# Two more seven-product joints in the middle of each layer, with the residual read again from DRAM

## The chip, the cores and the metric

One Trainium2 chip, one core. The time is the device time of one execution in microseconds. The kernel before takes 917.99 us (median of 3 runs, 916.48 to 919.03).

## The reference

A two-layer encoder on one sequence of 256 tokens with 2048 features, in float32. Cut to what matters:

```
for l in range(2):
    h = rmsnorm(x)                                  # 256 x 2048
    P = h @ w_in[l]                                 # 2048 x 7168, columns:
    a_x, a_b, a_c, a_g, d_q, d_k, d_v, d_g, m_q, m_g = split(P)
    #  768  768  768  768  768  768  768  768  512  512
    y_a = a_b * conv3(a_c * a_x) * silu(a_g)
    y_d = head_rms(diff_attention(norm(d_q), norm(d_k), d_v)) * silu(d_g)   # 6 heads, two softmaxes each
    y_m = mem_attention(norm(m_q), mem keys, mem values) * silu(m_g)        # 4 heads, 256 memory tokens
    x = x + concat(y_a, y_d, y_m) @ w_out[l]        # 2048 x 2048, the residual is x
```

## The kernel before

**Products.** TensorE (PE) works in fp32r, in which an fp32 number is split into a rounded part `hi` and a rest `lo`. Each fp32 product of a 128-token tile, a 128-row weight tile and 512 columns is three matmuls: hi·hi, hi·lo and lo·hi. `block` goes down the 16 row tiles of a weight matrix for 512 columns, two row tiles (a chunk) at a time. For each chunk SP issues a load of 512 KB into `raw` (a ring of 4, line L276), ACT rounds it into `hi` (L279), DVE subtracts to get `lo` (L280), both into a ring of 4 chunks, and PE does 12 matmuls (two row tiles, two token tiles, three each) at L290. Two accumulators of PSUM are used by a block.

**Seven products instead of eight.** For a pair of row tiles and two neighbouring column blocks, the function `seven` does a 2x2 block product with 7 products in place of 8 (21 matmuls of 512 columns for 24). It needs the following in return: two `wide` tiles (one row tile by 1024 columns each) in place of four ring chunks' halves; four subtractions of wide halves on DVE (`minus`, L365); splits of one half (`one`) and of three whole tiles (L362); sums of token tiles (`token_sums`), which are kept in rows 12 to 15 of `yT`, where the outputs of the four memory heads go later; and four more PSUM banks, x1 and x5 of pool `ps_s`, x6 and x7 of pool `ps_t`. These four are the banks that attention scores and attention outputs use at other times. A `joint` runs a block of the near columns with sevens put in at given row tiles (its `places`), then `collect` (L1048) adds x1, x6, x7 and x5 into four results `u`, and then the far columns' block runs on the row tiles that are left. `gather` (L1075) adds the `u` to the accumulators. Before, there are 10 sevens: in w_in in layer 0 one at place 8 of the first joint and two at 2 and 10 of the second, in layer 1 two at 4 and 10, all of them in the d columns at the layer's start; and five in w_out (2 and 3).

**Order of the program.** A layer's blocks of w_in are the d columns (six blocks), then the middle: C_M (memory queries), C_M+512 (memory gate), C_B, one with the rests of C_B and C_G, C_G, C_X, then C_C, and one with the rests of C_X and C_C. Then comes w_out. Beside the blocks run tasks: after each chunk `run_side` moves every task that is due (score and softmax of a pair of heads, normalisation, transposes, gates) by one step. A transpose goes through DRAM on SP's queue (`carry`: four writes at L470, such as `d<-sh`, and four reads at L474, such as `bgT<-d`). Most instructions are pinned to the order in which the program issues them; a scheduler orders the others.

**Attention beside it.** `pair` (three of them in each layer) runs two heads: 24 score matmuls (`s`, L582) into four banks of ps_s and ps_t, two `diff_weights` (L594 to L613: subtract the ALiBi, maximum, exp) with two steps between the heads, carry, and `weighted` into ps_t (`po`). Four memory heads follow with scores in ps_s and `po` in ps_t, and the outputs in yT.

**The residual.** `xs` is one resident tile of 128 x 2 x 2048 (16 KB of each partition). It holds mem at first, then x, is added to the w_out sums in place (L1282), and its squares give the next norm. At a layer's end `x_next` writes each quarter of it to DRAM for the transposes of the next layer.

Of the kernel before, what the change touches and what calls it, by code (L numbers as in the profile page):

```python
# [10 lines left out]
F32 = mybir.dt.float32  # L11
# [7 lines left out]
P = 128  # L19
# [5 lines left out]
W_MEM = 512  # L25
# [26 lines left out]
def encoder(ctx: ExitStack, tc: tile.TileContext, x, mem, norm_g, w_in, conv_w, conv_b,  # L52
# [34 lines left out]

    xs = const.tile([P, NT, D_MODEL], F32, name="xs")
    vb = tmp.tile([P, 2, B], F32, tag="yn", name="vb")
# [263 lines left out]
    def seven(stat, k, sums, rows, c_near, c_far, x, first, last, homes, meanwhile, single=(keep, "mga")):  # L353


        a, b = (pl.tile([P, 2, NB], F32, tag=tag, name=nm("wide")) for pl, tag in homes)
        for j, raw in enumerate((a, b)):
            pin(nc.sync.dma_start(raw.rearrange("p j c -> p (j c)"), rows(k + j)))

# [9 lines left out]

        one = single[0].tile([P, 2, 1, NB], F32R, tag=single[1], name=nm("one"))  # L370
        b11 = split(a[:, 0:1], (one[:, 0], one[:, 1]))
# [156 lines left out]

    held = {"e": 0, "sh": 0, "yn": 0}

    def pair(heads, begin, end, v):
# [27 lines left out]
        for i, h in enumerate(heads):  # L559
            end[0](h, yn[:, :, i], weighted(eT, i, v, h), *es[i][1:])  # L560
            yield 2
# [11 lines left out]
    def diff_scores(l, heads, yT):  # L573
        while not {(x, l, h) for x in "qk" for h in heads} <= made:
            yield 1
        scores = [[pl.tile([P, NT, SEQ], F32, tag=tag, name=nm("s")) for _ in range(2)]
                  for pl, tag in ((ps_s, "s"), (ps_t, "t"))]
        for h, s in reversed(list(zip(heads, scores))):
            for i in range(NT):
                for n, (a, b) in enumerate(((0, 1), (0, 0), (1, 0))):  # L580
                    for c, rows in enumerate(ROWS):
                        pin(nc.tensor.matmul(s[c][:, i, :], yT[rows, a, h, i * P:(i + 1) * P], yT[rows, b, CG + h, :],  # L582
                                             start=n == 0, stop=n == 2))
            scored.add((l, h))
        return scores
# [42 lines left out]
    def mem_scores(l, h, st):  # L628
# [8 lines left out]
        pin(nc.vector.scalar_tensor_tensor(kl, k, g, kh.bitcast(F32), ALU.mult, ALU.subtract))  # L637
        yield 1
        s = ps_s.tile([P, NT, SEQ], F32, tag="s", name=nm("s"))
        for i in range(NT):  # L640
# [21 lines left out]
    def mem_pair(l, n, st):  # L662
# [43 lines left out]
        yield 1  # L706
        for i, h in enumerate(heads):
            po = ps_t.tile([P, SEQ], F32, tag="t", name=nm("po"))
            at = 0
# [59 lines left out]
    def x_next(dst, l, q):  # L769

        d = dram.tile([NT, P, NB], F32, name=nm("xd"))
        tc.keep_in_program_order(nc.sync.dma_start(d.rearrange("t p c -> p t c"), xs[:, :, q * NB:(q + 1) * NB]))
        yield 2
        yield from x_turned(dst, l, q, d.rearrange("t p c -> (t p) c"))
# [12 lines left out]
    def x_square(c, t, pin=False):  # L787
        sq = tmp.tile([P, NB], F32, tag="nat", name=nm("sq"), bufs=3)
        i = nc.scalar.activation(sq, xs[:, t, c * NB:(c + 1) * NB], AF.Square, accum_out=ssx[:, t, c:c + 1])  # L789
        if pin:  # L790
            tc.keep_in_program_order(i)
# [8 lines left out]
    def mem_tokens(lo, n):  # L800
        return pin(nc.sync.dma_start(xs[:, :, lo:lo + n], mem[:, lo:lo + n].rearrange("(t p) c -> p t c", p=P)))

    def mem_columns(k, t):
        return xs[:, t, k * P:(k + 1) * P]

    def mem_squares(c):

        for t in range(NT):
            sq = tmp.tile([P, NB], F32, tag="nat", name=nm("msq"), bufs=3)
            pin(nc.scalar.activation(sq, xs[:, t, c * NB:(c + 1) * NB], AF.Square, accum_out=ssm[:, t, c:c + 1]))  # L810

# [24 lines left out]
    def x_natural(q):  # L836
        pin(nc.sync.dma_start(xs[:, :, q * NB:(q + 1) * NB],
                              x[:, q * NB:(q + 1) * NB].rearrange("(t p) c -> p t c", p=P)))
# [184 lines left out]
    for l in range(DEPTH):  # L1023
# [15 lines left out]

        def joint(b, places, homes, singles, home, **how):  # L1040
            near, far = accumulators(), accumulators()
            x = [pl.tile([P, NB], F32, tag=tag, name=nm("x"))
                 for pl, tag in ((ps_s, "s"), (ps_s, "s"), (ps_t, "t"), (ps_t, "t"))]
            u = keep.tile([P, 3, NB], F32, tag=home, name=nm("u"))
            us = [u[:, 0], u[:, 1], u[:, 2], tmp.tile([P, NB], F32, tag="yn", name=nm("u"))]

# [3 lines left out]
            def collect():  # L1050
                x1, x5, x6, x7 = x
                pin(nc.scalar.copy(us[0], x1))
# [4 lines left out]
                plus(us[3], us[1], x5)  # L1057

            def pair_at(n):
                def run(near):  # L1060
                    rows = lambda k: x_row_tiles(w_in[l], k, 1)[:, 0, C_D + b * NB:C_D + (b + 2) * NB]
                    seven(xT, 2 * n, summed[n], rows, near, far, x, n == 0, n == len(places) - 1,
                          homes[n], lambda: None, singles[n])
                    if n == len(places) - 1:
                        tasks.append(later(collect(), 1))
                    run_side(1)
                return run

            x_block([(C_D + b * NB, NB)], ALLK[2 * len(places):], acc=near, opened=(False, False),
                    between={c: pair_at(n) for n, c in enumerate(places)}, **how)  # L1070
            return near, far, us

        def gather(acc, us):
            for t in range(NT):
                nc.vector.tensor_tensor(us[t], acc[t], us[t], ALU.add)  # L1075
            return us

        def begin_pair(n, p):
# [15 lines left out]
        for b in order:  # L1094
# [7 lines left out]
            elif b in joints:  # L1102
                places = joints[b][0]
                acc, far, us = joint(b, *joints[b])
                finish = us[0:2]
            elif b - 1 in joints:
                acc = x_block([(C_D + b * NB, NB)], ALLK[2 * len(places):], acc=far, opened=(True, False))
                finish = us[2:4]
            else:
                acc = x_block([(C_D + b * NB, NB)], ready=m.ready if l == 0 and b == 0 else None)  # L1110

            def sums_of(acc=acc, us=finish):
                return gather(acc, us) if us else acc

# [30 lines left out]
        mga = sheet(keep, "mga")  # L1145
        acc = x_block([(C_M, NB)])

        def turn_mq(steps):
            nat = yield from steps
            yield 1  # L1150
# [3 lines left out]

        tasks.append(later(turn_mq(normed_steps(acc, P, st, sheets("bgx"))), LAG))
        acc = x_block([(C_M + W_MEM, NB)])

        def mem_gate(acc=acc):
            for t in range(NT):
                a = tmp.tile([P, NB], F32, tag="nat", name=nm("a"), bufs=3)  # L1160
# [68 lines left out]

        acc_b = x_block([(C_B, NB)])  # L1230
        soon(lambda: scaled(both_rows(bg, 0, 4), acc_b, HR2))
        acc_bg = x_block([(C_B + NB, 256), (C_G + NB, 256)])

        def last_gates():
            scaled(both_rows(bg, 4, 6), part(acc_bg, 0, 256), HR2)
            gate(NB, 256, part(acc_bg, 256, 256))

        soon(last_gates)
        acc_g = x_block([(C_G, NB)])
        soon(lambda: gate(0, NB, acc_g))  # L1240
        tasks.append(later(turn_bg(list(range(CG))), 9))
        acc_x = x_block([(C_X, NB)])
        ux = sheet(tmp, "e")
        soon(lambda: scaled(both_rows(ux, 0, 4), acc_x, R2))
        acc_c = x_block([(C_C, NB)])
# [27 lines left out]

        accs = [block(yT, w_out[l], [(b * NB, NB)], heads, more=True) for b in range(2)]
        final = l + 1 == DEPTH

        def finish(b, acc, keep_order=lambda i: i):
            for t in range(NT):
                n = 256 if final else NB
                for lo in range(0, NB, n):  # L1280
                    xc = xs[:, t, b * NB + lo:b * NB + lo + n]
                    keep_order(nc.vector.tensor_tensor(xc, acc[t][:, lo:lo + n], xc, ALU.add))  # L1282
# [25 lines left out]
        def collect(near):  # L1308

            def at(t, b):  # L1310
                return xs[:, t, b * NB:(b + 1) * NB]

# [21 lines left out]
        def pair_at(n):  # L1334
            def run(near):
                seven(yT, paired[n], sums[n], lambda k: w_out[l][k * P:(k + 1) * P, 2 * NB:4 * NB], near, far, x, n == 0, n == len(paired) - 1,
                      homes[n], (lambda: leave(1, accs[1], pin, 4)) if n == 0 else lambda: None)
# [40 lines left out]
```

## Time and profile before

| What | Value |
|---|---|
| median of 3 runs | 917.99 us (916.48 to 919.03) |
| the profiled execution | 917.21 us; the trace spans 915.4 us of it |
| granted TensorE clock, mean | 0.999 |
| PE busy | 909.6 us, 99% of the span |
| DVE busy | 672.4 us, 73% |
| ACT busy | 566.7 us, 62% |
| moved by DMA | 215.18 MB, mean 235 GB/s |

Busy times are sums of each engine's instructions. A matmul's record has about 390 ns and the next one starts before it ends, so PE's busy share says that PE has always something under way, and not how fast it is fed; the spacing between two starts tells that. In the chain that ended last, a piece "PE acc L290 x60" stands for sixty consecutive matmuls and their time.

### The profile page before, as it was taken

What the parts mean: (1) busy time and instruction counts of PE and PEld (TensorE: products, weight loads), DVE (VectorE), ACT (ScalarE), POOL (GpSimd) and SP (SyncE); (2) the same over time, 40 slices, a digit from 0 to 9 for tenths busy, and PEclk for the clock granted to TensorE, in tenths of its full rate; (3) what the DMA queues carried; (4) which work ended last, traced back from release to release, by engine and by line L of the source; (5) the groups of instructions that cost most, each with busy time, mean ns of one, the idle gap of its engine ahead of it and who ended that gap; (6) DMA issues with size and microseconds to landing.
All of it is one profiled execution on the core that took longest, in us unless ns stands there. A gap on an engine that the chain in (4) does not pass through costs nothing.

```text
span 915.4 us, 12589 instructions
## 1 busy us (share of the span) xinstructions
PE 909.6 (99%) x4194; PEld 751.5 (82%) x4194; DVE 672.4 (73%) x935; ACT 566.7 (62%) x1107; POOL 129.9 (14%) x187
## 2 busy tenths in 40 slices
PE   9999999999999999999999999999999999999998
PEld 6887888788888888888888888888888888888886
DVE  5558877987667667677689768876677578588786
ACT  5668865757757665545557656676666576456352
POOL 2376242200021010000000202120021010000000
PEclk9999999999999999999999999999999999999999
DMA  8898767777779898978776872887768999978842
GB/s 289 279 267 255 246 246 251 239 219 214 215 216 253 231 259 248 237 229 242 253 217 226 282 276 85 262 269 228 211 204 207 237 285 287 231 247 235 282 152 93
DMA packets 243282, 215.18 MB, mean 235 GB/s; under 512 B 131976, under 2 KB 171720, under 8 KB 243216
## 3 DMA queue, kind: packets, MB, share of 16 engines
q1 hardware_dynamic: 238240, 208.71, 76.5%
q0 software_dynamic: 3776, 4.59, 2.0%
q10 hardware_dynamic: 1200, 1.07, 0.3%
q8 instruction: 33, 0.54, 0.2%
q14 instruction: 33, 0.27, 0.1%
HBM read 193.30 MB, written 21.00 MB: 234 GB/s over the span
## 4 chain that ended last, share of the span: by engine, by line
PE 92%; DMA 2%; ACT 2%; DVE 2%; issue 1%; SPq 0%; ACTq 0%; DVEq 0%
PE acc L290 83%; PE x L336 3%; PE acc L336 2%; DMA raw<-in_w_mem_kv_dram 1%; PE po L491 1%; PE s L582 1%; DMA wide<-in_w_in_dram 1%; PE po L714 1%; DVE lo L280 1%; PE acc L894 1%; ACT sq L789 0%; ACT hi L876 0%; PE pt L728 0%; DMA d<-sh 0%; ACT sq L421 0%
## 5 line engine op out<-in xcount | busy, mean ns | idle before, releaser
L290 PE MATMUL acc<-hi,xT 128*128 128x512 f32 x1712 | 536.7, 390 | 0.0
L280 DVE TENSOR_TENSOR lo<-raw,hi 128x1024 fp32r<-128x1024 f32 x260 | 316.4, 1220 | 139.1 <-ACT hi L279 133.7
L279 ACT CAST hi<-raw 128x1024 fp32r<-128x1024 f32 x260 | 272.5, 1050 | 206.2 <-PE acc L290 164.6
L290 PEld LDWEIGHTS acc<-hi,xT 128*128 128x128 f32 x1712 | 321.3, 188 | 67.1 <-ACT hi L279 0.2
L290 PE MATMUL acc<-lo,xT 128*128 128x512 f32 x856 | 333.6, 390 | 0.3 <-DVE lo L280 0.3
L290 PEld LDWEIGHTS acc<-lo,xT 128*128 128x128 f32 x856 | 160.7, 188 | 32.8 <-DVE lo L280 0.7
L290 PE MATMUL acc<-hi,yT 128*128 128x512 f32 (+1 forms) x432 | 134.2, 388 | 0.0
L290 PEld LDWEIGHTS acc<-hi,yT 128*128 128x128 f32 x432 | 81.0, 188 | 16.8
L290 PE MATMUL acc<-lo,yT 128*128 128x512 f32 x216 | 83.7, 388 | 0.0
L290 PE MATMUL acc<-hi,memT 128*128 128x512 f32 x248 | 78.6, 393 | 0.0
L877 DVE SCALAR_TENSOR_TENSOR lo<-raw,cva,hi 128x1024 fp32r<-128x1024 f32 (+1 forms) x34 | 40.7, 1217 | 22.7 <-ACT hi L876 22.7
L290 PEld LDWEIGHTS acc<-hi,memT 128*128 128x128 f32 x248 | 46.1, 188 | 9.5 <-ACT hi L876 0.3
L290 PE MATMUL acc<-lo,memT 128*128 128x512 f32 x124 | 48.6, 392 | 0.1
L362 ACT CAST hi<-wide 128x1024 fp32r<-128x1024 f32 x30 | 31.2, 1048 | 26.4 <-DVE wide L365 10.7
L290 PEld LDWEIGHTS acc<-lo,yT 128*128 128x128 f32 x216 | 40.6, 188 | 8.4
L362 DVE TENSOR_TENSOR lo<-wide,hi 128x1024 fp32r<-128x1024 f32 x30 | 36.4, 1220 | 6.4 <-ACT hi L362 6.2
L876 ACT ACTIVATE hi<-raw,cva 128x1024 fp32r<-128x1024 f32 (+1 forms) x34 | 36.4, 1097 | 7.2 <-DMA raw<-in_w_mem_kv_dram 6.2
L424 POOL TENSOR_SCALAR ss<-ss,st 128x8 f32<-128x8 f32 (+1 forms) x16 | 14.6, 913 | 130.0 <-ACT sq L421 130.0
L187 POOL TENSOR_TENSOR rs<-ss,root 128x8 f32<-128x8 f32 (+1 forms) x20 | 32.0, 1601 | 1.7
L599 ACT ACTIVATE e<-e,mx 128x256 f32<-128x256 f32 x48 | 23.8, 498 | 9.6 <-DVE mx L594 9.6
L290 PEld LDWEIGHTS acc<-lo,memT 128*128 128x128 f32 x124 | 23.3, 188 | 6.0 <-DVE lo L877 1.2
L402 POOL TENSOR_SCALAR stt<-ssum 128x2 f32<-128x2 f32 x3 | 0.6, 188 | 186.3 <-DVE ssum L778 186.3
(213 smaller groups left out, 903.2 us busy)
## 6 DMA issues: line engine op xcount, KB each, us to landing
raw<-in_w_in_dram SPq DMA_DIRECT2D x182, 512.0 KB, 4.6
raw<-in_w_out_dram SPq DMA_DIRECT2D x54, 512.0 KB, 4.7
raw<-in_w_in_dram SPq DMA_DIRECT2D x64, 256.0 KB, 3.7
raw<-in_w_mem_kv_dram SPq DMA_DIRECT2D x30, 512.0 KB, 5.8
d<-sh SPq DMA_DIRECT2D x88, 128.0 KB, 4.3
sh<-d SPq DMA_DIRECT2D x72, 128.0 KB, 3.8
wide<-in_w_in_dram SPq DMA_DIRECT2D x10, 512.0 KB, 5.9
wide<-in_w_out_dram SPq DMA_DIRECT2D x10, 512.0 KB, 5.9
```

Of the source, the lines that this page charges most:

```text
L187: nc.gpsimd.tensor_tensor(r, t, root[:, 0:n], ALU.pow)
L279: nc.scalar.copy(hi, raw)
L280: nc.vector.tensor_tensor(lo_, raw, hi.bitcast(F32), ALU.subtract)
L290: i = nc.tensor.matmul(acc, left, right, start=start, stop=stop)
L336: nc.tensor.matmul(acc, left[a], right[b], start=first and i == 0, stop=last and i == 2)
L362: return ((hi, pin(nc.scalar.copy(hi, src))), (lo, pin(nc.vector.tensor_tensor(lo, src, hi.bitcast(F32), ALU.subtract))))
L424: nc.gpsimd.tensor_scalar(ss[:, t], ss[:, t], 1.0 / gs, col(st, ET, t), ALU.mult, ALU.add)
L491: nc.tensor.matmul(po[:, t, :], eT[:, i, t, k, :], v[:, k, h * P:(h + 1) * P], start=k == 0, stop=k == NT - 1)
L582: pin(nc.tensor.matmul(s[c][:, i, :], yT[rows, a, h, i * P:(i + 1) * P], yT[rows, b, CG + h, :], start=n == 0, stop=n == 2))
L599: nc.scalar.activation(e[:, c, i], e[:, c, i], AF.Exp, bias=mx[:, c, i:i + 1], scale=-1.0, accum_out=sm[:, c, i:i + 1])
L876: both = (nc.scalar.activation(hi[:, j], raw[:, j], AF.Copy, scale=g), nc.vector.scalar_tensor_tensor(lo[:, j], raw[:, j], g, hi[:, j].bit ...
L877: nc.vector.scalar_tensor_tensor(lo[:, j], raw[:, j], g, hi[:, j].bitcast(F32), ALU.mult, ALU.subtract))
```

## The change

The residual is no longer resident. A pool `quarters` of four tiles (the bytes of `xs`) holds, one after the other, the quarters of mem, the quarters of x for layer 0's squares, and in each layer's middle the wide tiles, the `one` parts and the results `u` of two new joints. Then, after each of the first two w_out blocks, two quarters of the residual are read from DRAM (512 KB each): x itself in layer 0, the copy that `x_next` wrote in layer 1. The new joints are C_M with C_M+512 and C_G with C_X, each with sevens at row tiles 2 and 8, in both layers: 8 sevens more, 18 in all. The wide tiles of C_G and C_X come in two pieces.

Two flags order the attention around them. While a joint holds the four banks, `held["closed"]` keeps scores, `weighted` and the memory heads from starting. `held["sums"]` keeps the memory heads' outputs, which overwrite the token sums in yT, until both joints have run. In `pair` both heads' `diff_weights` are issued one after the other and followed by 8 steps.

```diff
-    xs = const.tile([P, NT, D_MODEL], F32, name="xs")
+    quarters = pool("quarters", 4)
+    xs, xd = {}, {}
...
+    held = {"e": 0, "sh": 0, "yn": 0, "closed": 0, "sums": 0}
     def pair(heads, begin, end, v):
...
             es.append(begin[1](h, s))
-            yield 2
-        yield 4
+        yield 8
...
-        while held["yn"] == 2:
+        while held["yn"] == 2 or held["closed"]:
             yield 1
...
     def diff_scores(l, heads, yT):
-        while not {(x, l, h) for x in "qk" for h in heads} <= made:
+        while held["closed"] or not {(x, l, h) for x in "qk" for h in heads} <= made:
...
+            while held["closed"] or held["sums"]:
+                yield 1
             po = ps_t.tile([P, SEQ], F32, tag="t", name=nm("po"))
...
+        def block_pair(cols, far_cols, places):
+            if not places:
+                near, far = x_block(cols), []
+                yield lambda: near
+                far = x_block(far_cols)
+                yield lambda: far
+                return
+            near, far, us = joint(cols, far_cols, places)
+            yield lambda: gather(near, us, 0)
+            x_block(far_cols, ALLK[2 * len(places):], acc=far, opened=(True, False))
+            yield lambda: gather(far, us, NT)
...
-        acc = x_block([(C_M, NB)])
+        mid = ((2,8),(),(2,8)) if l == 0 else ((2,8),(),(2,8))
+        held["sums"] = sum(1 for places in mid if places)
+        these = block_pair([(C_M, NB)], [(C_M + W_MEM, NB)], mid[0])
+        acc = next(these)
...
-        acc_g = x_block([(C_G, NB)])
+        these = block_pair([(C_G, NB)], [(C_X, NB)], mid[2])
+        acc_g = next(these)
...
-        accs = [block(yT, w_out[l], [(b * NB, NB)], heads, more=True) for b in range(2)]
+        accs = []
+        for b in range(2):
+            accs.append(block(yT, w_out[l], [(b * NB, NB)], heads, more=True))
+            for q in (2 * b, 2 * b + 1):
+                xs[q] = quarter()
+                pin(nc.sync.dma_start(xs[q], xd[l, q]))
```

How the order of instructions moves at three places. Lines of the changed kernel are some 5 to 7 further down: L280 is L285 there, L290 is L295, L365 is L371, and the sevens' matmuls are at L341 and the splits of their wide tiles at L368.

DVE in layer 1, at the block of C_M. Before, its first lo tiles, and between them and the next the softmax of the first head pair (`e`, from the score banks `s`):

```order
L280 TENSOR_TENSOR lo_5987<-raw_5984,hi_5986 128x1024
L280 TENSOR_TENSOR lo_6005<-raw_6002,hi_6004 128x1024
L522 SCALAR_TENSOR_TENSOR yT_4785<-sh_5714,kgain,yT_4785 128x1024
L594 ISA e_5897,mx_5898<-s_5867,al_5895 128x256
L594 ISA mx_5898 128x1
```

After, the first seven of the joint's last split (lo_6128), then a key's gain, a gate and the second head's softmax, and only then the lo of the next ordinary chunk (lo_6161):

```order
L368 TENSOR_TENSOR lo_6124<-xq_6106,hi_6123 128x1024
L613 TENSOR_TENSOR e_5995<-e_5995 128x512
L487 SCALAR_TENSOR_TENSOR ga_5165<-th_6176,acc_5832 128x512
L368 TENSOR_TENSOR lo_6128<-xq_6107,hi_6127 128x1024
L528 SCALAR_TENSOR_TENSOR yT_4879<-sh_5812,kgain,yT_4879 128x1024
L487 SCALAR_TENSOR_TENSOR ga_5165<-th_6179,acc_5833 128x512
L601 ISA e_6017,mx_6018<-s_5967,al_6015 128x256
...
L285 TENSOR_TENSOR lo_6161<-raw_6158,hi_6160 128x1024
```

The softmax of that head and the seven's own work, which were apart, now stand in a row ahead of one chunk.

PE at the same place. Before, the chunks of C_M follow each other:

```order
L290 MATMUL acc_5983<-lo_5987,xT_4037 128x512
L290 MATMUL acc_5983<-hi_5986,xT_4037 128x512
L290 MATMUL acc_5982<-hi_6004,xT_4037 128x512
L290 MATMUL acc_5982<-lo_6005,xT_4037 128x512
L290 MATMUL acc_5982<-hi_6004,xT_4037 128x512
```

After, the seven's products into x7 and x6 (x_6105, x_6104), whose banks the second head's scores held, stand behind two hi matmuls of the next chunk:

```order
L341 MATMUL acc_6081<-hi_6127,xT_4111 128x512
L295 MATMUL acc_6080<-hi_6160,xT_4111 128x512
L295 MATMUL acc_6081<-hi_6160,xT_4111 128x512
L341 MATMUL x_6105<-hi_6123,yT_4879 128x512
L341 MATMUL x_6105<-lo_6124,yT_4879 128x512
L341 MATMUL x_6105<-hi_6123,yT_4879 128x512
L341 MATMUL x_6104<-hi_6127,yT_4879 128x512
L341 MATMUL x_6104<-lo_6128,yT_4879 128x512
L341 MATMUL x_6104<-hi_6127,yT_4879 128x512
L295 MATMUL acc_6080<-lo_6161,xT_4111 128x512
```

So PE comes to the lo of the next chunk eight matmuls after its own seven.

SP's queue in layer 0, from the block of C_C into the last one (whose loads come in two halves, "x2"). Before, each carry has two loads around it:

```order
L470 DMA d_3791<-sh_2730 32x4x384 x4
L276 DMA raw_3798<-in_w_in_dram 128x2x512
L276 DMA raw_3824<-in_w_in_dram 128x2x512
L474 DMA bgT_3678<-d_3791 128x12x32 x4
L276 DMA raw_3848<-in_w_in_dram 128x2x256 x2
L276 DMA raw_3881<-in_w_in_dram 128x2x256 x2
```

After, three carries (that of b's columns, that of a memory head and that of u) write and read back within four loads:

```order
L476 DMA d_3885<-sh_2726 32x4x384 x4
L476 DMA d_3890<-yn_3488 32x4x128 x4
L281 DMA raw_3897<-in_w_in_dram 128x2x256 x2
L476 DMA d_3916<-sh_3772 32x4x256 x4
L281 DMA raw_3925<-in_w_in_dram 128x2x256 x2
L480 DMA bgT_3769<-d_3885 128x12x32 x4
L480 DMA yn_3488<-d_3890 128x4x32 x4
L281 DMA raw_3960<-in_w_in_dram 128x2x256 x2
L480 DMA sh_3772<-d_3916 128x8x32 x4
L281 DMA raw_3987<-in_w_in_dram 128x2x256 x2
```

Counted over the program, matmuls of 512 columns go from 3807 to 3783, DVE's rows from 922 to 1001 and SP's from 411 to 419.

More of the change, by code (lines that the diff above doesn't have):

```diff
@@ L353, in seven @@
     def seven(stat, k, sums, rows, c_near, c_far, x, first, last, homes, meanwhile, single=(keep, "mga")):
-        a, b = (pl.tile([P, 2, NB], F32, tag=tag, name=nm("wide")) for pl, tag in homes)
+        a, b = (pl.tile([P, 2, NB], F32, tag=tag, name=nm("wide")) for pl, tag in homes) if homes else (quarter(), quarter())
         for j, raw in enumerate((a, b)):
-            pin(nc.sync.dma_start(raw.rearrange("p j c -> p (j c)"), rows(k + j)))
+            for to, of in rows(k + j):
+                pin(nc.sync.dma_start(raw.rearrange("p j c -> p (j c)")[:, to], of))
         def split(src, to=None):
@@ L368, in side_of @@
             return [v[:, j] for v, _ in parts]
-        one = single[0].tile([P, 2, 1, NB], F32R, tag=single[1], name=nm("one"))
+        one = single[0].tile([P, 2, 1, NB], F32R, tag=single[1], name=nm("one")) if single else quarter(F32R, (2, 1, NB))
         b11 = split(a[:, 0:1], (one[:, 0], one[:, 1]))
@@ L559, in pair @@
         for i, h in enumerate(heads):
+            while held["closed"]:
+                yield 1
             end[0](h, yn[:, :, i], weighted(eT, i, v, h), *es[i][1:])
@@ L638, in mem_scores @@
         yield 1
+        while held["closed"]:
+            yield 1
         s = ps_s.tile([P, NT, SEQ], F32, tag="s", name=nm("s"))
@@ L1038, in x_sums, with joint @@
             yield from token_sums(xT, 2 * n, home)
[L1040 to L1045, printed above, removed]
+        def joint(cols, far_cols, places, homes=None, singles=None, home=None):
+            near, far, x = accumulators(), accumulators(), []
+            us = []
             def plus(dst, v, u):
@@ L1051, in collect @@
                 x1, x5, x6, x7 = x
+                if home:
+                    u = keep.tile([P, 3, NB], F32, tag=home, name=nm("u"))
+                    us.extend([u[:, 0], u[:, 1], u[:, 2], tmp.tile([P, NB], F32, tag="yn", name=nm("u"))])
+                else:
+                    u = quarter(), quarter()
+                    us.extend(u[i][:, t] for i in range(2) for t in range(NT))
                 pin(nc.scalar.copy(us[0], x1))
@@ L1067, in pair_at, with gather @@
                 return run
-            x_block([(C_D + b * NB, NB)], ALLK[2 * len(places):], acc=near, opened=(False, False),
-                    between={c: pair_at(n) for n, c in enumerate(places)}, **how)
+            x_block(cols, ALLK[2 * len(places):], acc=near, opened=(False, False),
+                    between={c: pair_at(n) for n, c in enumerate(places)})
             return near, far, us
-        def gather(acc, us):
+        def gather(acc, us, at):
+            assert us
+            us = us[at:at + NT]
             for t in range(NT):
@@ L1103, in encoder @@
                 places = joints[b][0]
-                acc, far, us = joint(b, *joints[b])
-                finish = us[0:2]
+                acc, far, us = joint([(C_D + b * NB, NB)], [(C_D + (b + 1) * NB, NB)], *joints[b])
+                finish = us, 0
             elif b - 1 in joints:
                 acc = x_block([(C_D + b * NB, NB)], ALLK[2 * len(places):], acc=far, opened=(True, False))
-                finish = us[2:4]
+                finish = us, NT
             else:
@@ L1112, in sums_of @@
             def sums_of(acc=acc, us=finish):
-                return gather(acc, us) if us else acc
+                return gather(acc, *us) if us else acc
             if b == 3:
@@ L1153, in turn_mq @@
             queries[l] = mqT, keep.tile([P, 6, SEQ], F32R, tag="bgT", name=nm("parts"))
-        tasks.append(later(turn_mq(normed_steps(acc, P, st, sheets("bgx"))), LAG))
-        acc = x_block([(C_M + W_MEM, NB)])
+        tasks.append(later(turn_mq(acc), LAG))
+        acc = next(these)
         def mem_gate(acc=acc):
+            acc = acc()
             for t in range(NT):
@@ L1335, in run @@
             def run(near):
-                seven(yT, paired[n], sums[n], lambda k: w_out[l][k * P:(k + 1) * P, 2 * NB:4 * NB], near, far, x, n == 0, n == len(paired) - 1,
+                seven(yT, paired[n], sums[n], lambda k: [(slice(0, 2 * NB), w_out[l][k * P:(k + 1) * P, 2 * NB:4 * NB])], near, far, x, n == 0, n == len(paired) - 1,
                       homes[n], (lambda: leave(1, accs[1], pin, 4)) if n == 0 else lambda: None)
```

60 lines of the change are left out of this document (41 added, 19 removed).

## The prediction

> **What bounds the kernel now.** I read the page's busy times first, then the chain, then what PE waited for, and last PE's own spacing.
>
> ```profile
> span 915.4 us, 12589 instructions
> PE 909.6 (99%) x4194; PEld 751.5 (82%) x4194; DVE 672.4 (73%) x935; ACT 566.7 (62%) x1107; POOL 129.9 (14%) x187
> PE 92%; DMA 2%; ACT 2%; DVE 2%; issue 1%; SPq 0%; ACTq 0%; DVEq 0%
> PE warm L131 <- DVE zeros L126: 1.2, 1, 1.2
> PE acc L894 <- ACT hi L876: 0.6, 1, 0.6
> PE acc L290 <- DVE lo L280: 0.3, 1, 0.3
> ```
>
> PE is on the chain for 92% of the span, and its waits (engine, line, releaser: total, times, longest) come to 2.1 us, 0.9 of them behind the start. So PE's stream sets the time, and the question is how much of its work goes away and whether the others still feed it. Its pace, from the chain (start, length, engine, line, count), the second piece first by length:
>
> ```profile
> 263.85 13.63 PE acc L290 x60
> 572.16 57.12 PE acc L290 x252
> ```
>
> 13.63/60 and 57.12/252 are 0.227 us for each matmul of 512 columns, and a chunk of 12 takes 2.73 us. ACT and DVE run ahead as far as their ring of four parts lets them:
>
> ```profile
> L280 DVE TENSOR_TENSOR lo<-raw,hi 128x1024 fp32r<-128x1024 f32 x260 | 316.4, 1220 | 139.1 <-ACT hi L279 133.7
> L279 ACT CAST hi<-raw 128x1024 fp32r<-128x1024 f32 x260 | 272.5, 1050 | 206.2 <-PE acc L290 164.6
> ```
>
> ACT's largest idle time is for PE to leave a ring place (164.6 us). A part is then ready 1.05 + 1.22 us after its place came free, and PE reaches it three chunks after that point: 3 x 2.73 - 2.27 = 5.9 us of lead. That lead is the cushion of which everything below is paid. It is used up where DVE has more than 2.73 us of work for each 2.73 us of PE's.
>
> **The sum, part by part.** It is made against the profiled execution, 917.21 us (span 915.4 and 1.8 around it), which lies 0.78 under the median of the runs.
>
> *A, the eight sevens.* Each has 21 matmuls where two normal row tiles have 24, so 24 fewer of 0.227 us: -5.45 us, all of it on PE and so on the path.
>
> *B, score runs that split.* With the new flags and the eight steps in a row, PE's order has three more places in which a pair's run of scores is cut by matmuls of 512 columns (two in layer 1, one in layer 0). Before there is one such place, in layer 1:
>
> ```profile
> 686.11 0.39 PE L290 MATMUL acc<-hi,xT 128*128 128x512 f32 x1
> 686.43 0.38 PE L582 MATMUL s<-yT 64*128 64x256 f32 x1
> 686.74 0.50 PE L290 MATMUL acc<-hi,xT 128*128 128x512 f32 x1
> 687.07 0.40 PE L290 MATMUL acc<-lo,xT 128*128 128x512 f32 x1
> 238.42 1.62 PE s L582 x24
> ```
>
> From the first of these starts to the last are 0.96 us. Two matmuls of 512 columns at 0.227 and one score at 1.62/24 = 0.068 (last row, an uncut run from the chain) would be 0.52. A cut costs 0.44 us, three cost +1.3.
>
> *C, DVE in the four new joints.* A seven has four subtractions and 3.5 splits on DVE in place of two chunks' splits, and a joint has four additions in `collect` and four in `gather` besides:
>
> ```profile
> L365 DVE TENSOR_TENSOR wide<-wide 128x512 f32<-128x512 f32 x20 | 13.8, 692 | 0.6
> L362 DVE TENSOR_TENSOR lo<-wide,hi 128x1024 fp32r<-128x1024 f32 x30 | 36.4, 1220 | 6.4 <-ACT hi L362 6.2
> L362 DVE TENSOR_TENSOR one<-wide,one 128x512 fp32r<-128x512 f32 x10 | 6.9, 687 | 4.6 <-ACT one L362 4.5
> L1048 DVE TENSOR_TENSOR u<-u,x 128x512 f32<-128x512 f32 x12 | 7.9, 679 | 1.9 <-PE x L336 1.9
> L1075 DVE TENSOR_TENSOR u<-acc,u 128x512 f32<-128x512 f32 x12 | 8.0, 683 | 0.0
> ```
>
> A seven: 4 x 0.692 + 3 x 1.220 + 0.687 = 7.12 us against 2 x 1.22 = 2.44, so 4.68 more. PE's 21 matmuls take 4.77, so each seven eats at least 2.35 us of the lead. A joint: 2 x 4.68 + 4 x 0.679 + 4 x 0.683 = 14.8 us more, four joints 59, and DVE rises from 672 to 731 us, 80% of the span. On the average that is covered. Locally the nearest measured case is layer 1's joint with places 4 and 10:
>
> ```profile
> 546.00:573.00 27.00, 27.00 (x121) 22.30 (x120) 23.36 (x30) 18.91 (x49) 6.65 (x4) 1.00 0.35 120
> 569.23 0.68 DVE L431 TENSOR_TENSOR sh<-acc,rs 128x512 f32<-128x512 f32 x1
> 570.57 1.23 DVE L280 TENSOR_TENSOR lo<-raw,hi 128x1024 fp32r<-128x1024 f32 x1 [0.65 <-ACT hi L279]
> ```
>
> The window's columns are PE, PEld, DVE and ACT busy (and counts), POOL, clock, DMA share and GB/s. DVE is busy for 23.36 of 27 us there, and the lo that ends at 571.80 comes 0.4 us ahead of the chunk that begins at 572.16 in the chain above. No wait, but nothing left. One foreign instruction more is enough, as in layer 0's first joint, where the chain crosses to DVE:
>
> ```profile
> 170.23 0.68 DVE sh L431
> 170.91 1.15 DVE lo L280
> 172.10 8.50 PE acc L290 x36
> ```
>
> A normalisation of 0.68 us stands ahead of the lo, and PE waits 0.3 (the third row of the waits). In the d columns the joints have little else beside them. The new ones stand where attention runs:
>
> ```profile
> 636.00:658.00 22.00, 22.00 (x115) 18.11 (x114) 15.05 (x18) 14.52 (x26) 0.44 (x2) 1.00 0.64 205
> L594 DVE CUSTOM_DVE_ANT_0 e<-s,al 128x256 f32<-128x256 f32 x48 | 17.1, 420 | 1.2 <-PE s L582 1.2
> L594 DVE DVE_READ_ACCUMULATOR2_ANT mx<- 128x1 f32 x48 | 4.0, 83 | 0.0
> L606 DVE TENSOR_TENSOR e<-e 128x512 f32<-128x512 f32 x12 | 8.2, 684 | 0.5 <-ACT e L605 0.4
> L481 DVE SCALAR_TENSOR_TENSOR ga<-th,acc 128x512 f32<-128x512 f32 (+1 forms) x6 | 3.5, 596 | 1.4 <-ACT th L480 1.4
> L522 DVE SCALAR_TENSOR_TENSOR yT<-sh,kgain,yT 128x512 fp32r<-128x512 f32 (+1 forms) x4 | 4.1, 1014 | 0.1
> ```
>
> In layer 1's C_M block (around 636 to 658) DVE has 15.05 of 22 us today, and 19.7 with one seven. The new order puts into one row, between the lo of the chunk ahead of the first seven and that of the chunk behind it: the seven's 7.12 us, both heads' softmax (8 x (0.420 + 0.083) = 4.0), factors and a product (0.37, an estimate from rows of some 0.2, and 0.68), two gates (2 x 0.60), a key's gain (about 1.25, the larger form of the last row), and the lo itself: 15.9 us. PE has 12 + 21 + 2 matmuls until it needs it, 7.9 us. The lead there is longer than 5.9, since PE is held up ahead of it for 1.62 us by the scores: up to 7.5. 15.9 - 7.9 - 7.5 = 0.5, and 0.6 when I walk through it instruction by instruction. In the C_G joints a memory head's score and softmax and a gate (some 3 us) lie between the sevens, and x5 waits for that head's maximum and exp: 3 + 2.35 us taken of 5.9 for the first seven, and the second comes before the lead has come back. By the same walk 0.8 us in each layer. Layer 0's C_M joint has its softmaxes apart: 0. Sum +2.2. The ends are 0 (the joint at 546, full and without a wait) and about 7: one wait of 3.6 in layer 1's C_M joint (softmax of 4.0 against a margin of 0.4), and in the other three the longest wait that PE has anywhere, 1.2. I take 2.2, nearer to the row without a wait, since three of the four meet less than a softmax.
>
> *D, SP's queue.* b's carry, a memory head's and u's now write and read within four loads ahead of and in the last block of w_in, in both layers. Of before I read (start, length, issues) and the issue times by line (min/median/max in ns):
>
> ```profile
> 371.21 2.73 SPq L470 DMA_DIRECT2D d<-sh  x4
> 378.11 6.10 SPq L474 DMA_DIRECT2D bgT<-d  x4
> 735.47 5.29 SPq L474 DMA_DIRECT2D sh<-d  x4
> L470 SPq DMA_DIRECT2D d<-sh x104: 303/458/1152, 149.2 to 831.1; - x104
> L474 SPq DMA_DIRECT2D sh<-d x72: 366/582/3502, 154.1 to 778.5; - x72
> raw<-in_w_in_dram SPq DMA_DIRECT2D x182, 512.0 KB, 4.6
> ```
>
> Three writes (2.73 + 2 x 4 x 0.458 = 6.4), three reads (6.10 + 2 x 4 x 0.58 = 10.7) and eight half loads of about 0.4 (3.1) are 20.2 us of SP, and 23 if one read is as long as that of 5.29. PE needs 10.9 for four chunks. The difference of 9.3 to 12 meets the lead of 5.9 and the head start of the raw ring, 4 x 2.73 - 2.27 - 4.6 (landing, last row) - 0.4 = 3.7 us: 9.6 in all. So nothing is left over, or 2.4 a layer. I take +0.3, near the lower end, because the medians stand for more rows; ends 0 and 5.
>
> *E, the residual read again.* 4.2 MB more on 215, eight loads of 512 KB and no arithmetic. Rows: xs and raw loads take 6.5 and 4.7 us to land.
>
> ```profile
> xs<-in_x_dram SPq DMA_DIRECT2D x4, 512.0 KB, 6.5
> raw<-in_w_out_dram SPq DMA_DIRECT2D x54, 512.0 KB, 4.7
> ```
>
> Two stand behind each head block of w_out, needed tens of microseconds later. Two loads ahead of a weight load delay it by up to 2 x (6.5 - 4.7) = 3.6 us by sharing, within the lead of 5.9 where nothing else presses on DVE: 0, ends 0 and 1 (the memory outputs, which come later now, end close to w_out's start). The pool's own waits are costless for the same reason: a quarter comes free long before.
>
> Sum: 917.21 - 5.45 + 1.3 + 2.2 + 0.3 + 0 = 915.6, and with 0.78 for the median 916.3. I write 916.2.
>
> **A rule beside it.** The Trainium skill, "Perfetto Trace Analysis", section "Identifying the Most-Contended Engine", says to find the engine with the highest occupancy and to improve that one first, and to judge PE by the share of weight loads and not of matmuls. By both (99% and 82% here, DVE 73%) PE comes first, and less work on PE would then be a gain of its full 5.45 us: 912.5. It knows no cushion between engines, and the row at 172.10 shows one that ran out at less than full DVE. "DMA: Bandwidth & Descriptors", section "Issuing engines are not separate DMA queues", calls the sequencer's time to initiate a DMA usually small against the DMA itself. By that D is 0. The row of 6.10 us for four issues, whose data take about 4 us to land, disagrees.
>
> **Rivals.** R1: the joints keep feeding PE as the one at 546 does, and C and D vanish. Then A and B alone are left, 917.99 - 5.45 + 1.3 = 913.8, and 912.5 if the cuts also hide. For it speaks that joint with 23.36 of 27; against it the 0.3 us at 172 and the softmax of 4.0 us that this joint has not beside it. R2, slower: the pile on SP's queue. If the lead is still down to 2 us when it comes, because the second joint's far block has not given it back, a layer pays 23 - 10.9 - 3.7 - 2 = 6.4 us, both 12.8: 916.0 + 12.8 = 928.8. It decides (above 920.7) once D reaches 4.7, that is with a lead under 6 in both layers and reads at their longest, or under 3.2 at the medians. For it the row of 6.10; against it that 24 chunks lie between the last seven and the pile, and each gives back up to 2.73 - 1.22 us. R3: C at its upper end, 7 instead of 2.2: 921.1. That the change doesn't do what it says is out: the order has 24 fewer matmuls of 512 columns.
>
> **How the numbers follow.** About 0.3%, 2.75 us, can be told from no change here: 915.24 to 920.74. Forecast (waits of 1.4 to 6.9 us in C and D together) 0.52, R1 (under 1.4) 0.38, R2 0.06, R3's part above the bound 0.04. So faster 0.38, same 0.52, slower 0.10. The range reaches down to 913.3, R1's price less the spread of the runs, and up to 919.8, where C and D cost 6; below and above lie about 1 in 10 each.
>
> **What the profile after would show.** A: PE's matmuls 24 fewer, its share 99%. B: score runs (s at L589) cut by L295 in four places, each with 0.4 us more. C: in the chain "DVE lo L285" or L368 ahead of PE in C_M of layer 1 and in both C_G joints, 0.6 to 0.8 each, and no wait in layer 0's C_M. D: PE waits for DVE or ACT in the block of halves ahead of w_out, released by a late raw load, under 0.5 a layer. E: none at w_out's start. The prediction is wrong if the total of PE's waits stays at 2 us (R1) or if waits of over 2 us stand ahead of the last block of w_in in both layers (R2).

## The result and the profile after

The changed kernel takes 927.45 us (median of 6 runs, 926.6 to 930.48) against 918.04 for the kernel before on the same chip: a ratio of 1.0112, 95% interval 1.0094 to 1.013. It is slower by 1.1%. Two executions of the experiments below, 1306.54 us in e1 and 1851.21 us in e6, are slow ones and left out of the medians, and as they were the profiled ones, no profile of these two is read. The prediction had 916.2, within 0.3% of before, and gave a slower kernel 1 chance in 10.

The head of the page after, with PE's share of the chain, answers to the first rows shown of before:

```profile
span 924.8 us, 12700 instructions
PE 911.1 (99%) x4170; PEld 748.6 (81%) x4170; DVE 719.5 (78%) x1015; ACT 579.3 (63%) x1127; POOL 128.7 (14%) x187
PE 78%; DMA 7%; DVE 6%; SPq 4%; ACT 2%; issue 2%; POOL 0%; ACTq 0%; DVEq 0%
```

PE has 24 matmuls fewer (4170 for 4194) and is still "busy" for 99%. The chain shows the difference: PE carries 78% of it and no longer 92%, and SP's queue, which had 0%, has 4%, DMA 7%. PE's waits (engine, line, releaser: total, times, longest):

```profile
PE acc L295 <- ACT hi L284: 5.1, 3, 3.9
PE x L341 <- ACT hi L368: 1.3, 1, 1.3
PE warm L136 <- DVE zeros L131: 1.2, 1, 1.2
PE acc L295 <- DVE lo L285: 1.1, 3, 0.5
```

One wait of 3.9 us stands out. It is in layer 0, in the last block of w_in. Here are PE's rows around it, and then a table of windows there (start:end, length, then PE, PEld, DVE, ACT and POOL busy, the granted clock, the DMA share, GB/s):

```profile
399.26 0.39 PE L295 MATMUL acc<-lo,xT 128*128 128x512 f32 x1
399.49 0.39 PE L295 MATMUL acc<-hi,xT 128*128 128x512 f32 x1
403.77 1.22 PE L295 MATMUL acc<-hi,xT 128*128 128x512 f32 x2 [3.90 <-ACT hi L284]
405.62 0.63 PE L295 MATMUL acc<-hi,xT 128*128 128x512 f32 x1
406.05 0.63 PE L295 MATMUL acc<-lo,xT 128*128 128x512 f32 x1
```

```profile
403.80:407.00 3.20, 3.16 (x7) 2.06 (x8) 2.47 (x4) 0.95 (x2) 0.00 (x0) 0.50 0.94 227
407.00:410.10 3.10, 3.10 (x10) 2.13 (x8) 1.21 (x2) 2.18 (x4) 0.00 (x0) 0.61 0.95 294
410.10:413.00 2.90, 2.90 (x13) 2.43 (x14) 2.90 (x6) 2.54 (x3) 0.00 (x0) 1.00 1.06 361
```

PE ran out of parts at 399.7 and began again at 403.77. From there its matmuls start 0.43 us apart (405.62, 406.05) and not 0.227, and the granted clock is 0.50, then 0.61, and 1.00 only from about 410 on. So the wait was paid nearly twice.

What PE waited for is seen on SP's queue (start, length, issues):

```profile
370.75 7.28 SPq L281 DMA_DIRECT2D raw<-in_w_in_dram  x3
378.07 4.17 SPq L476 DMA_DIRECT2D d<-sh  x4
382.29 2.56 SPq L476 DMA_DIRECT2D d<-yn  x4
384.95 0.92 SPq L281 DMA_DIRECT2D raw<-in_w_in_dram  x2
385.97 1.94 SPq L476 DMA_DIRECT2D d<-sh  x4
388.00 1.04 SPq L281 DMA_DIRECT2D raw<-in_w_in_dram  x2
389.22 5.81 SPq L480 DMA_DIRECT2D bgT<-d  x4
395.08 2.95 SPq L480 DMA_DIRECT2D yn<-d  x4
398.13 0.96 SPq L281 DMA_DIRECT2D raw<-in_w_in_dram  x2
399.14 3.75 SPq L480 DMA_DIRECT2D sh<-d  x4
```

From 378.07 to 398.13 SP issued two chunks' loads (x2 is one chunk in two halves), 5.5 us of PE's work, and 20 small transfers. The third chunk's load was issued at 398.13, landed at 402.6, and PE began 1.05 us of ACT later.

To add the difference up I took the time from each matmul's start to the next and subtracted the undisturbed spacing (0.227 us for 512 columns). The excess over the kernel before, by stage: 7.4 us in the last block of layer 0's w_in (4.1 for the wait, the rest the slow clock and 0.2 or so of DVE), 3.1 in the same place of layer 1, 2.0 in layer 1's w_out, 2.3 in the two stages with the joints. With -5.45 for the matmuls that is +9.4, as the spans have it (915.4 to 924.8).

The wait in layer 1's w_out is at the first seven. ACT gets the wide tile late (after, then before):

```profile
864.16 0.93 SPq L364 DMA_DIRECT2D wide<-in_w_out_dram  x2
872.74 0.62 ACT L368 CAST one<-wide 128x512 fp32r<-128x512 f32 x1 [0.16 <-DMA wide<-in_w_out_dram]
880.27 1.61 ACTq L1347 DMA_DIRECT2D out_dram<-xq  x2
881.98 1.99 ACT L368 CAST hi<-wide 128x1024 fp32r<-128x1024 f32 x2 [5.11 <-DMA out_dram<-xq]
```

```profile
859.20 0.94 SPq L358 DMA_DIRECT2D wide<-in_w_out_dram  x2
862.79 0.62 ACT L362 CAST one<-wide 128x512 fp32r<-128x512 f32 x1
864.59 1.05 ACT L362 CAST hi<-wide 128x1024 fp32r<-128x1024 f32 x1 [1.19 <-PE acc L290]
```

Before, the tile was there 3.6 us after SP's row began. After, 8.6 us passed. The sums of the block ahead with the residual also came later on DVE (879.50, before 869.31), and ACT's two output transfers, which wait for them, stand ahead of the casts, as they did before (870.10).

### The profile page after: what moved, and what is told of

It reads as the page before. It is cut to its first block, busy times and chain, and to the rows that moved or that the text cites. A ratio compares the mean times of both kernels' runs of the same rounds, so it can differ in the third digit from the quotient of the medians.

```text
span 924.8 us, 12700 instructions
## 1 busy us (share of the span) xinstructions
PE 911.1 (99%) x4170; PEld 748.6 (81%) x4170; DVE 719.5 (78%) x1015; ACT 579.3 (63%) x1127; POOL 128.7 (14%) x187
## 4 chain that ended last, share of the span: by engine, by line
PE 78%; DMA 7%; DVE 6%; SPq 4%; ACT 2%; issue 2%; POOL 0%; ACTq 0%; DVEq 0%
PE acc L295 66%; PE x L341 4%; PE acc L341 3%; DMA raw<-in_w_out_dram 3%; DVE lo L285 2%; DMA raw<-in_w_in_dram 2%; SPq L480 2%; SPq L476 1%; PE s L589 1%; ACT hi L284 1%; PE po L497 1%; DVE lo L368 1%; DMA wide<-in_w_in_dram 1%; PE acc L912 1%; ACT hi L368 0%
## 5 line engine op out<-in xcount | busy, mean ns | idle before, releaser
L295 PE MATMUL acc<-hi,xT 128*128 128x512 f32 x1584 | 499.5, 392 | 5.1 <-ACT hi L284 5.1
L285 DVE TENSOR_TENSOR lo<-raw,hi 128x1024 fp32r<-128x1024 f32 x244 | 294.9, 1217 | 101.1 <-ACT hi L284 100.4
L284 ACT CAST hi<-raw 128x1024 fp32r<-128x1024 f32 x244 | 254.1, 1049 | 163.5 <-PE acc L295 75.2
L295 PEld LDWEIGHTS acc<-hi,xT 128*128 128x128 f32 x1584 | 298.0, 189 | 68.5 <-ACT hi L284 6.8
L295 PE MATMUL acc<-lo,xT 128*128 128x512 f32 x792 | 310.4, 392 | 1.1 <-DVE lo L285 1.1
L295 PEld LDWEIGHTS acc<-lo,xT 128*128 128x128 f32 x792 | 149.3, 188 | 33.3 <-DVE lo L285 3.1
L295 PE MATMUL acc<-hi,yT 128*128 128x512 f32 (+1 forms) x432 | 134.2, 388 | 0.0
L295 PEld LDWEIGHTS acc<-hi,yT 128*128 128x128 f32 x432 | 81.0, 188 | 16.7
L295 PE MATMUL acc<-lo,yT 128*128 128x512 f32 x216 | 83.7, 388 | 0.0
L295 PE MATMUL acc<-hi,memT 128*128 128x512 f32 x248 | 78.5, 392 | 0.0
L295 PEld LDWEIGHTS acc<-hi,memT 128*128 128x128 f32 x248 | 46.2, 188 | 9.3
L368 ACT CAST hi<-wide 128x1024 fp32r<-128x1024 f32 x30 | 31.1, 1046 | 28.1 <-DVE wide L371 13.2
L295 PE MATMUL acc<-lo,memT 128*128 128x512 f32 x124 | 48.3, 389 | 0.0
L295 PEld LDWEIGHTS acc<-lo,yT 128*128 128x128 f32 x216 | 40.6, 188 | 8.4
L368 DVE TENSOR_TENSOR lo<-wide,hi 128x1024 fp32r<-128x1024 f32 x30 | 36.5, 1221 | 8.1 <-ACT hi L368 7.9
L368 ACT CAST hi<-xq 128x1024 fp32r<-128x1024 f32 x24 | 25.2, 1050 | 19.9 <-DVE xq L371 15.9
L430 POOL TENSOR_SCALAR ss<-ss,st 128x8 f32<-128x8 f32 (+1 forms) x16 | 12.4, 775 | 178.4 <-ACT sq L427 178.4
L368 DVE TENSOR_TENSOR lo<-xq,hi 128x1024 fp32r<-128x1024 f32 x24 | 29.3, 1220 | 0.6 <-ACT hi L368 0.4
L341 PE MATMUL x<-hi,yT 128*128 128x512 f32 x78 | 28.8, 390 | 0.0
```

The lines of the kernel that those rows point to most:

```text
L284: nc.scalar.copy(hi, raw)
L285: nc.vector.tensor_tensor(lo_, raw, hi.bitcast(F32), ALU.subtract)
L295: i = nc.tensor.matmul(acc, left, right, start=start, stop=stop)
L341: nc.tensor.matmul(acc, left[a], right[b], start=first and i == 0, stop=last and i == 2)
L368: return ((hi, pin(nc.scalar.copy(hi, src))), (lo, pin(nc.vector.tensor_tensor(lo, src, hi.bitcast(F32), ALU.subtract))))
L430: nc.gpsimd.tensor_scalar(ss[:, t], ss[:, t], 1.0 / gs, col(st, ET, t), ALU.mult, ALU.add)
```

## The experiments

Theory Q: SP's queue issues in order, and since the memory heads' outputs now wait for both joints (they overwrite the token sums), their carry falls onto those of b and u. The weight loads behind them are late. Theory E: the residual's reads, in pairs next to the conv's carries, take what lead is left in w_out. Rivals: R, the 4.2 MB more themselves; D, DVE's work in the joints wears the lead down.

### No joints, one pair of joints, and b's carry earlier

One chip and shared runs of the kernel before (917.81 us). First, all four joints off:

```diff
-        mid = ((2,8),(),(2,8)) if l == 0 else ((2,8),(),(2,8))
+        mid = ((),(),()) if l == 0 else ((),(),())
```

> The changed kernel without the four new joints: the residual is still read from DRAM at w_out, the quarters pool and the pair's eight steps stay, no seven is added. Theory Q (SP's queue: the memory heads' carry, held back by the token sums, falls onto b's and u's carries, so that weight loads are issued late in the last block of w_in): the carries stand apart here as in the kernel before, so PE does not wait there, and the time is 918 to 920, the upper end if the reads at w_out cost the 2 us that the trace after shows in layer 1's w_out. Rival R (traffic: the residual's 4.2 MB and their place take the time): 922 or more. Rival D (DVE worn down by the joints): 917 to 918.5.

Run e1: 918.1 us, ratio 1.0006 (0.9994 to 1.0018). The reads and the pool alone cost nothing that can be measured. R falls; the time fits Q and D alike. This kernel also has the wide tiles of the d columns in two pieces of 256 KB (20 issues for 10), as the changed kernel has: there all wide tiles of w_in come so, and not those of C_G and C_X alone.

Joints at C_M only:

```diff
+        mid = ((2,8),(),()) if l == 0 else ((2,8),(),())
```

> Joints only at C_M and C_M+512 in both layers, C_G and C_X as ordinary blocks: 4 sevens more than before, 12 matmuls fewer. The memory heads are released after the first joint. Theory Q: two carries instead of three meet in the last stage, 10 to 11 us of the pile are gone with the memory heads' one, time 916 to 919. Rival R: 922 or more. Rival D: the C_M joint beside the softmaxes keeps half of the loss, 921 to 923.

Run e2: 919.58 us, ratio 1.0027 (1.0013 to 1.0042), a little above the range for Q. In its profile no wait of over 0.4 us is left in w_in's last block, and the loss sits in w_out: 2.2 us in layer 0, 1.2 in layer 1.

Joints at C_G only:

```diff
+        mid = ((),(),(2,8)) if l == 0 else ((),(),(2,8))
```

> Joints only at C_G and C_X in both layers: also 4 sevens more. The memory heads' outputs still wait for this joint, so their carry still falls with b's and u's, six groups of four issues among six loads instead of among four. Theory Q: the larger part of the loss stays, 920 to 926, with PE waiting in the last block of w_in. Rival R: 922 or more, as in the run without joints. Rival D: half of the loss, 921 to 923, with the waits spread over the joint and not in the last block.

Run e3: 930.84 us, ratio 1.0142 (1.0118 to 1.0166): slower than with all four joints, which no theory had. The pile costs 2.6 us in layer 0 and 1.9 in layer 1, and w_out 2.1 and 3.2. But 7.0 us are lost in layer 1's C_G joint, at the first seven. Its chain (start, length, what):

```profile
738.84 0.91 PE po L497 x8
739.77 0.41 ACT hz L623 x3
740.75 0.70 POOL ht L192
742.37 0.52 ACT xq L368
742.91 0.70 DVE xq L368
743.64 0.70 DVE xq L371
```

The head's normalisation goes from PE to ACT to POOL and back to ACT, and the cast of the seven's `one` (ACT xq) stands behind it on ACT's queue. PE waits 3.2 us, and the clock is at half behind it again (0.50 and 0.52 from 743 to 749). With all four joints the heads lie otherwise and this doesn't occur.

Then the test of Q itself: all four joints, and one number changed.

```diff
-        tasks.append(later(turn_bg(list(range(CG))), 9))
+        tasks.append(later(turn_bg(list(range(CG))), 4))
```

> All four joints and all else as in the changed kernel, but the transposition of b's columns becomes due 4 chunks after the gate instead of 9, so its four writes and four reads on SP's queue are issued some four weight loads ahead of the memory heads' and u's. Nothing else is taken away. Theory Q: the waits of 7.4 us (layer 0) and 3.1 us (layer 1) ahead of and in the last block go away almost wholly, time 916.5 to 919. Rivals R and D: only the order of small transfers has changed, 924 to 928.

Run e4: 921.38 us, ratio 1.0042 (1.0027 to 1.0057), 6 us under the changed kernel's. The waits in the last blocks are gone (excess 0.7 and 0.0 us, from 7.4 and 3.1). The median lies 2.4 us above Q's range. The profile is of the shortest of the ten executions (918.9 us; the longest took 924.87), which is itself inside the range; what is left over in it is w_out, 2.8 us in layer 0 and 2.1 in layer 1, and 0.8 in layer 0's C_G joint. That w_out also keeps the median up is borne out by the next experiment. The chain of its profile shows there, among other pieces:

```profile
435.33 8.67 DMA raw<-in_w_out_dram
456.31 8.69 DMA xd<-xq
466.88 6.05 DMA wide<-in_w_out_dram
479.54 0.50 PE acc L341
```

A raw load lands 8.7 us after its issue behind two residual reads. Block 0 ends later, its quarter's write to DRAM (xd) ends at 465, and the wide load stands on SP's queue behind the reads that wait for it.

### The residual one quarter at a time

```diff
-            for q in (2 * b, 2 * b + 1):
-                xs[q] = quarter()
-                pin(nc.sync.dma_start(xs[q], xd[l, q]))
+        def residual(q):
+            xs[q] = quarter()
+            pin(nc.sync.dma_start(xs[q], xd[l, q]))
+            yield
+        for q, n in enumerate((4, 9, 19, 22)):      # ahead of the last block of w_in
+            tasks.append(later(residual(q), n))
```

> e4 (b's transposition due 4 chunks after the gate) and, besides, the residual's four quarters read one at a time: one behind each of the 4th, 9th, 19th and 22nd chunks counted from the last block of w_in, in place of two pairs behind the two head blocks of w_out, where the conv's carries are. In e4's profile what is left over the kernel before is 2.7 us in layer 0's w_out and 2.1 in layer 1's (loads of raw and wide tiles that land 6 to 9 us after issue), 0.8 in the C_G joint of layer 0, 1.3 in cut score runs. Theory E (pairs of residual reads next to carries make the weight loads land late and w_out's sevens have no lead to spare): the 4.8 us of w_out shrink to under 1.5 and the time is 914.5 to 917, at least 3 us under e4's 921.4. Rival L (w_out starts with less lead because the memory heads end later; the reads are innocent): 920 to 922, as e4.

Run e5: 916.82 us against 917.37: ratio 0.9997 (0.9987 to 1.0008), 4.6 us under e4 (4.1 when each is set against the kernel before on its own chip). w_out has no wait left in either layer, and E holds against L. One of 1.0 us remains where the first quarter is read among w_in's last loads.

> The kernel of e1 again (residual read at w_out, no new joints), for a profile of its w_out at full clock. Theory E: the same pairs of reads make raw loads land late here too, so DVE's lead ahead of w_out's sevens is below that of the kernel before and PE waits there for up to 1 us, less than in e4 only because nothing else came before; time 917 to 919. Rival L: no wait and the same landing times as in the kernel before (median 4.7 us).

Run e1b: a single execution, 916.77 us. There is no wait in w_out, though loads land late here too:

```profile
raw<-in_w_out_dram SPq DMA_DIRECT2D x54, 512.0 KB, 5.7
wide<-in_w_out_dram SPq DMA_DIRECT2D x10, 512.0 KB, 8.2
```

Before they took 4.7 (the row shown there) and 5.9. So neither theory has all of it: E's wait did not come, and L's equal landing times did not hold. I compared when each lo was ready with when PE first used it: before, the lead is 5.5 to 5.9 us from 415 to 463; here it falls to 3.5 behind the first pair of reads and to 0.6 behind the sevens' parts (at 483.7), with nothing lost; in e4 it is at 0.4 behind the first pair. So both matter. The reads alone take 2.4 us of lead, which costs nothing where the lead is whole. In e4 the last matmuls of the memory heads' outputs come at 417 (399 here), and DVE splits their operands among the los up to 406, where the lead is under 1 us. It is back at 5.2 ahead of the pair, but SP's queue is then later for PE's pace: its first reads of uT start 1.9 us ahead of w_out's first matmul, 5.1 here. In e2, which lies between, they start 2.9 us ahead, and the lead behind the pair is 1.2. That it is the memory heads that put the queue behind is argued from this; no run changes them alone.

### Where the pile's time is, and both remedies

First, b early and the quarters behind the 16th, 19th, 21st and 23rd chunks, none of them among w_in's last loads:

```diff
+        for q, n in enumerate((16, 19, 21, 23)):
```

> As e5 (b's transposition early, residual read one quarter at a time), but the quarters behind the 16th, 19th, 21st and 23rd chunks from the last block of w_in, so that none is among that block's last weight loads. In e5 one wait of 1.0 us (1.9 with its neighbours) is left at the start of w_out, 0.7 in e4. Theory E': the first quarter's read among the last loads of w_in costs that 1.2 us; 914.5 to 916.5, 0.5 to 1.5 under e5's 916.8. Rival: DVE's own work there (gates, sums, normalisation) makes the wait, and nothing changes: 916.5 to 917.5.

Run e6: 915.02 us against 917.72, ratio 0.9971 (0.9959 to 0.9982): inside the range of E', with a gain of 1.8 over e5 where up to 1.5 was expected. All four reads have moved, and not the first alone, so the time agrees with E' and does not prove it. Then the changed kernel with b's carry issued by another queue:

```diff
-            yield from turn_sheet(bg[:, :, g0:g1], bgT[:, g0:g1])
+            yield from turn_sheet(bg[:, :, g0:g1], bgT[:, g0:g1], eng=nc.gpsimd)
```

> The changed kernel with one edit: the eight transfers of b's carry are issued by POOL's queue instead of SP's, at the same place in the program and with the same bytes (residual in pairs as in the changed kernel). Theory Q (issue time on SP's queue, in order, is what makes the weight loads late): the waits ahead of and in w_in's last block vanish as in e4, 918.5 to 922.5. Rival B (the small packets of three carries keep the DMA engines themselves busy, whoever issues them): 925 to 928.

Run e7: 919.54 us, ratio 1.0017 (1.0003 to 1.003), 8 us under the changed kernel, with an excess of under 0.3 us in each of the last blocks. This run alone does not rule out B. The same bytes move, but the four reads of bgT start 10 us earlier (379.2 for 389.2), and the profile books POOL's transfers on another DMA queue: 3.15 MB more on q0 in 1,024 packets, for 13,568 fewer on q1, SP's. What speaks against B is the changed kernel's own trace. The second half of the third chunk's load, issued behind the pile's writes and most of its reads, landed in 3.95 us (first row, from the chain), and the median of that size is 4.0 (second row; 3.7 before):

```profile
398.63 3.95 DMA raw<-in_w_in_dram
raw<-in_w_in_dram SPq DMA_DIRECT2D x64, 256.0 KB, 4.0
```

The load was late because it was issued late, and the DMA engines were not slow. So the cost was the issue time on SP, in order ahead of the loads. The remaining loss is w_out's (2.9 us in layer 0, 0.5 in layer 1) and 1.0 us in layer 0's C_G joint.

> The changed kernel with b's transposition as it is (due after 9 chunks, so the pile on SP stays) and only the residual read as in e6. Theory Q with E': the 7.4 and 3.1 us in w_in's last block stay, the 2 us in layer 1's w_out go: 923.5 to 926. Rival (waits in the last block and w_out are one thing, and go together): 917 to 919, or 927 if neither goes.

Run e8: 923.35 us, ratio 1.0066 (1.0052 to 1.008), just under the lower edge of Q's range. Its profile has 6.3 and 3.9 us in the two last blocks and none in w_out. The two costs are separate: this one with only the pile, e7 with only the reads in pairs, and the next with neither.

> e7 and e6 together: b's carry on POOL's queue and the residual one quarter at a time. Theory Q with E': no wait of over 1 us behind the joints; 24 matmuls fewer show, less the cut score runs of 1.3 and about 0.6 in layer 0's C_G joint: 913.5 to 916, under the kernel before. Rival B: 923 or more.

Run e9: 913.87 us against 917.72: ratio 0.9958, interval 0.9945 to 0.9971. It is the best kernel here, 0.4% under the one before. Its span and all of PE's waits:

```profile
span 911.1 us, 12713 instructions
PE warm L136 <- DVE zeros L131: 1.2, 1, 1.2
PE acc L295 <- DVE lo L285: 0.3, 1, 0.3
PE acc L913 <- ACT hi L895: 0.2, 1, 0.2
```

All are older than the change: the start, and the 0.3 us at about 171. 911.1 is 4.3 under the 915.4 of before, but 1.0 of that lies ahead of the first matmul of w_in (at 97.90 us, before at 98.92; it varies from 97.4 to 98.9 over the profiles here). PE's stream behind it is 3.1 us shorter: 5.45 for the matmuls, less 1.3 for the cut score runs and about 1.0 in pieces of 0.2 or so over the joints' stages. On POOL's queue the b carry takes its time beside SP's loads:

```profile
373.88 2.29 POOL L477 DMA_DIRECT2D d<-sh  x4 [9.09 <-DVE sh L459]
377.12 4.15 POOL L481 DMA_DIRECT2D bgT<-d  x4 [0.96 <-DMA d<-sh]
```

## Why the prediction was wrong

**A held.** 24 matmuls fewer are 5.45 us. In e9, 3.9 us faster than the kernel before by the medians, they show, less B and small pieces.

**B held.** The cuts are at four places, and one looks as before (s at 255.72 starts 0.31 ahead of the next row). From 255.41 to 256.60 are 1.19 us for three matmuls of 512 columns and one score, which uncut would take 0.75: 0.44 for a cut, as forecast.

```profile
255.41 0.39 PE L295 MATMUL acc<-hi,xT 128*128 128x512 f32 x1
255.72 0.38 PE L589 MATMUL s<-yT 64*128 64x256 f32 x1
256.03 0.73 PE L295 MATMUL acc<-hi,xT 128*128 128x512 f32 x2
256.60 0.39 PE L295 MATMUL acc<-lo,xT 128*128 128x512 f32 x1
```

**C was too dear on the whole.** It had 2.2 us: 0.6 in layer 1's C_M joint and 0.8 in each C_G joint. In the changed kernel there is 0.4 in layer 0's C_G joint (0.6 in e5, 0.8 in e4, 1.0 in e7, none in e9, so there the 0.8 is about right) and, besides the cuts, none of over 0.3 elsewhere in the joints. DVE went to 719.5 us, not 731, and it was not what limited. On this term R1 was nearer, and D, the rival of the experiments, was wrong: e4 keeps all the joints' DVE work and is 6 us faster.

**D failed, and it decided.** It had +0.3 for both layers, with ends 0 and 5; 10.5 was measured. Three things were wrong in it. First the shape: it set the whole pile (20.2 us) against four chunks, as if loads and carries were evenly mixed. What counts is what stands ahead of one load. Ahead of the third load are three writes, two loads and two of the three reads: by the prediction's own durations 6.4 + 1.6 + 6.1 + 2.3 = 16.4 us against 5.5 of PE's, 10.9 against a cushion of 9.6, so 1.3 and not nothing. Second the durations: issued in a crowd, the three writes took 4.17 + 2.56 + 1.94 = 8.7 us and not 6.4, and the stretch 20.1. 20.1 - 5.5 - 9.6 = 5.0; the wait was 3.9. The medians over the program did not hold here. Third, the clock: the sum had no price for a long wait beyond its length. Some 3 us of layer 0's 7.4 are matmuls at half clock.

R2 named this mechanism and this place, and priced it at 928.8, near the 927.45 measured. But its condition, a lead worn down to 2 us by the joints, was not what happened: the lead was 6.3 us at 391.8. Its chance of 0.06 rested on that condition. That its total comes within 1.4 us is luck: it had 12.8 for the pile where 10.5 was measured, kept C's 2.2, and had nothing for the 2.0 in w_out.

**E failed by 2 us.** Ends 0 and 1 were given, for a lead of 5.9 "where nothing else presses on DVE". The reads cost nothing alone (e1). In layer 1 of the changed kernel the pile and the memory heads, which the same change made late, had left a lead of 0.6 at 822. It was back at 5.4 by 839, and the pair of reads took it to 0.8 by 846, which is 4.6 where the reads alone took 2.4 (e1b). The prediction saw the later end and did not carry it into the price: each cost was set against the full cushion by itself.

**The rules beside it.** Against the rule on the sequencer's time (the Trainium skill, "DMA: Bandwidth & Descriptors", section "Issuing engines are not separate DMA queues", which calls it usually small) the prediction set a row of 6.10 us, and the row was right. Its "about 4 us to land" was not: those reads of bgT land in 6.0 in the median, so the four issues take as long as one of the transfers. Less work on the fullest engine was a gain only once the queue was cleared, and then 2.7 (e6) and 3.9 us (e9) of the 5.45. On the clock, the Trainium skill's "TensorE: Matmul & The Clock Gate", section "HAM oscillation — how this bites in real kernels", says that a wait for a DMA that crosses the activity monitor's window throttles PE, so that the next work starts cold. The traces agree: clocks of 0.50 behind the waits of 3.9 us here and 3.2 in e3 (that one for ACT and not for a DMA), and 1.00 behind those of 1.3 us and less.

## What to carry to other kernels

Small transfers that shared an in-order queue with the loads which feed the bound engine cost their issue time here. Count, for each load, what stands ahead of it, at the longer of the durations measured, and set that against the lead once, together with everything else that draws on the same lead. When a change delays a step, look where that step's transfers fall on the queue now. A few issues on an idle engine's queue, or one step's due time, can decide whether a gain in work shows.

## What was not expected of the hardware

A wait of 3.9 us cost PE its full clock for about 6.3 us more (403.8 to 410.1), and so 3 us beyond its own length. In e8 PE starts again at 402.4 behind a wait of 3.2 us and has its usual spacing from 407.1 on, 4.7 us later. One of the six executions of the changed kernel kept a mean clock of 1.000 and still took 929.45 us, so the half clock is not a fixed part of the loss. And the same four reads of bgT took 5.81 us of SP's queue in the changed kernel and 4.15 on POOL's in e9.
